# A two-layer diffusion trunk in one program: another instruction order, an output projection in eight blocks, another form for the weights' low parts

## The chip, the cores and the metric

The kernel runs on one core of a Trainium2 chip. The metric is the device time of one execution in microseconds (us); less is better. Times are medians of several executions; the profile is that of one execution, taken by the hardware profiler.

## The reference

One step through a trunk of two layers over 384 tokens (128 context, 256 latent), width 1024, everything in float32. A layer is a SwiGLU with half a residual, a token mixing of three head groups side by side, and a second SwiGLU; each is preceded by an RMS norm with a shift, a scale and a gate that come from a conditioning vector.

```python
def trunk_layer(x, mod, lp, lam_init, ctx=None, pos=None):
    sh1, sc1, g1, sh2, sc2, g2, sh3, sc3, g3 = (mod[:, i] for i in range(N_MOD))
    h = modulate(rms_norm(x, lp['g_norm'][0]), sh1, sc1)
    x = x + 0.5 * g1[:, None, :] * swiglu(h, lp['w_ffn_gate'][0], lp['w_ffn_up'][0], lp['w_ffn_down'][0])
    h = modulate(rms_norm(x, lp['g_norm'][1]), sh2, sc2)
    mix, new_ctx = token_mix(h, lp, lam_init, ctx, pos)
    x = x + g2[:, None, :] * mix
...
def token_mix(h, lp, lam_init, ctx, pos):
...
    out_c = diff_attention(c_q, keys_c, vals_c, lam)
    out_c = (rms_norm(out_c, lp['g_c_out']) * (1.0 - lam_init)).reshape(B, T, C_WIDTH)
    out = jnp.concatenate([out_a, out_b, out_c], axis=-1) @ lp['w_out']
```

Group a is grouped-query attention (384 columns of the concatenation), b a gated linear attention (256), c a differential attention of four heads of 96 columns (384): 1024 in all, eight times 128.

## The kernel before, in words

Six stages follow one another: FFN (0,0), mixing 0, FFN (0,1), FFN (1,0), mixing 1, FFN (1,1). Activations lie with features on the partitions and the 384 tokens along the free axis. Weights stream from memory in tiles of up to 128 x 1024. To keep float32 accuracy, every large product is three matmuls (`mm3`, L308 to L310): weight and activation are each split into a rounded high part and the rest. `load_split` does this for weights: a DMA on the SyncE queue (L299), the high part `whi` by ScalarE (L303), the low part `wlo = raw - whi` by VectorE (L304). Five raw buffers and three each of high and low parts stand in turn. While FFN stages run, VectorE also computes the conditioning vectors from `araw` tiles (L254).

At a stage's start TensorE begins with matmuls on `u`, the activation without its norm (`make_u`), since the norm's factor isn't known yet. `make_rstd` computes that factor: a matmul of ones on the summed squares `acc` (L377), a VectorE transpose (L379), three Newton steps on small tiles (`newton`, L315 to L327), a second transpose (L382). In mixing, `make_h` then makes the normed activation: GpSimd multiplies (L391), ScalarE writes the high part, VectorE shifts and scales (L397) and subtracts (L403). Projections onto 288, 384 and 512 columns (matmuls `<-whi,h`) need these; the four `t5` tiles (L604) are `u` products times the factor. In the FFN the first products are scaled by L464 and L469.

The mixing's second half is attention: queries times keys (L789 for group c), maximum (L694), exponential (L697), transposes (L721), values (L801, L803). `ORDER` gives the order in which the mixing's pieces are written for each layer. `c_first`, `c_next`, `c_norm` and `c_split` treat group c's output: two pairs of heads, each pair normed and split into four blocks of 96 rows in all.

The output projection multiplies nine blocks (three of a, two of b of 128 rows, four of c of 96 rows) for each of eight output tiles; `KORD` gives their order in the sum. Weights come in two loads a tile, of 640 and 512 columns. The order of instructions on an engine is what the tile framework's scheduler makes of the order in which they are written; each engine runs its queue in order.

Of the kernel before, what the change touches and what calls it, by code (L numbers as in the profile page):

```python
# [17 lines left out]
P = 128  # L18
D = 1024
KT = 8  # L20
SEQ = 128
LAT = 256
T = SEQ + LAT
# [23 lines left out]
TW = T + 2  # L47
# [7 lines left out]
NPT = 3  # L55
# [5 lines left out]
NRM = (0, 1)  # L61
HV = (1, 1, 1, 1, 1, 1, 1, 1)
ORDER = (
    ("ha br bq hb bk wq bv lg rq de wk st L0 rk L1 cx wa wv L2 c0 L3 c1 L4 c2 ra L5 L6 n0 s0 c3 n1 p0 ax "
     "s1 go o0 p1 p2 o1 o2").split(),
    ("br ha hb bq bk bv lg L0 wq rq wk de L1 st rk L2 wa cx wv L3 c0 ra L4 c1 c2 L5 c3 n0 L6 p0 ax "
     "go o0 p1 s0 p2 o1 n1 s1 o2").split(),
)
KORD = (
    ("c0 c1 c2 c3 b0 b1 a0 a1 a2").split(),  # L70
    ("a0 b0 b1 c0 c1 a1 c2 c3 a2").split(),
)


def build(tc, ins, outs):
    nc = tc.nc
    ctx = ExitStack()
    with ctx:
        _build(ctx, tc, nc, ins, outs)


def _build(ctx, tc, nc, I, O):
    V, S, G, PE = nc.vector, nc.scalar, nc.gpsimd, nc.tensor
# [3 lines left out]
    hp = ctx.enter_context(tc.tile_pool(name="hp", bufs=NHP))  # L87
# [208 lines left out]

    def load_split(src, cols=WCOL):
        raw = wp.tile([P, WCOL], F32, tag="wraw", bufs=NRAW, name="wraw")
        di = nc.sync.dma_start(out=raw[:, :cols] if len(src.shape) == 2 else  # L299
                               raw[:, :cols].rearrange("p (j c) -> p j c", j=src.shape[1]), in_=src)  # L300
# [260 lines left out]
    def mixing(l, us, acc, nxt):  # L561
        turn["own"] = {"mm": ("both",), "ax": ("ada",)}
        r_ = make_rstd(acc)
        with tc.tile_pool(name=f"mix{l}", bufs=1) as mp:
            def mt(shape, tag, bufs=1, dt=F32):
                return mp.tile(shape, dt, tag=tag, bufs=bufs, name=tag)
# [9 lines left out]
            s0 = mt([P, 2, 64], "s0")  # L576
# [6 lines left out]
            gco = sp[:, S_GCO + l:S_GCO + l + 1]  # L583
# [43 lines left out]
            c0, c1 = c01  # L627
# [107 lines left out]
            moa = []  # L735
# [14 lines left out]
            def a_out(i, pts):  # L750
                po = (mmps if PMM[6 + i] else axps)()[:, :T]
                for k in range(4):
                    for g in range(2):
                        r = slice(64 * g, 64 * g + 64)
                        if k == 0:
                            PE.matmul(po[r, 0:P], lhsT=av[:, 0, r], rhs=ptx[:, g, i, :], start=True, stop=True)
                        else:
                            PE.matmul(po[r, P:T], lhsT=av[:, k, r], rhs=pts[g][:, k - 1, :],  # L758
                                      start=(k == 1), stop=(k == 3))
                hi = hp.tile([P, TW], F32R, tag="h", name="ohi")[:, :T]  # L760
                S.activation(out=hi, in_=po, func=AF.Copy)
                lo = hp.tile([P, TW], F32R, tag="h", name="olo")[:, :T]
                V.tensor_tensor(out=lo, in0=po, in1=hi.bitcast(F32), op=ALU.subtract)
                moa.append((P, hi, lo))


            ptc_ = []
# [13 lines left out]
            moc = []  # L781
# [28 lines left out]
            cp = {}  # L810

            def c_first(j):
                cp[j] = mt([P, 2, T], "oc", 2)[:96], mt([P, 2, T], "pt", NPT)[:96], []
                c_next(j, 0)

            def c_next(j, i):
                oc, osq, pss = cp[j]
                c_head(2 * j + i, oc[:, i, :], osq[:, i, :], pss)

            def c_norm(j):  # L820
                oc, osq, pss = cp[j]
                r = rsq_bcast(mp, pss, T, 1.0 / 96, 96, "c", osq, osq)
                V.scalar_tensor_tensor(out=oc, in0=oc, scalar=gco[:96], in1=r, op0=ALU.mult, op1=ALU.mult)

            def c_split(j):
                oc = cp[j][0]
                for i in range(2):
                    hi = hp.tile([P, TW], F32R, tag="h", name="chi")[:96, :T]
                    S.activation(out=hi, in_=oc[:, i, :], func=AF.Copy)
                    lo = hp.tile([P, TW], F32R, tag="h", name="clo")[:96, :T]  # L830
                    V.tensor_tensor(out=lo, in0=oc[:, i, :], in1=hi.bitcast(F32), op=ALU.subtract)
                    moc.append((96, hi, lo))


            bv = mt([P, 3, 256], "bv")
            de = mt([P, 8, P], "de")
# [108 lines left out]
            def gla_out():  # L945
                ot = mt([P, 2, T], "e", 3)
                for i in range(2):
                    po = [(mmps if PMM[9] else axps)()[64 * j:64 * j + 64, :T] for j in range(2)]
                    for c in range(3):
                        for step in range(3 if c else 1):  # L950
                            for j in range(2):
                                h = 2 * i + j
                                r = slice(32 * h, 32 * h + 32)
                                pc = po[j][:, c * P:(c + 1) * P]
                                if step == 0:
                                    PE.matmul(pc, lhsT=bv[:, c, 64 * h:64 * h + 64], rhs=sc[i][:, j, c, :],
                                              start=True, stop=(c == 0))
                                elif step == 1:
                                    PE.matmul(pc, lhsT=s0[r, 0, :] if c == 1 else st[r, 0, :], rhs=de[r, c - 1, :],
                                              start=False, stop=False)  # L960
                                else:
                                    PE.matmul(pc, lhsT=st[r, 1, :] if c == 1 else s0[r, 1, :], rhs=de[r, c + 1, :],
                                              start=False, stop=True)
                    for j in range(2):
                        S.activation(out=ot[64 * j:64 * j + 64, i, :], in_=po[j], func=AF.Copy)
                oq = mt([P, 2, T], "e", 3)
                S.activation(out=oq, in_=ot, func=AF.Square)
                pss = []
                for i in range(2):
                    ps = (mmps if PMM[15] else axps)()[:, :T]  # L970
                    PE.matmul(ps, lhsT=bones, rhs=oq[:, i, :], start=True, stop=True)
                    pss.append(ps)
                r = rsq_bcast(mp, pss, T, 1.0 / 64, P, "b", oq, mt([P, 2, T], "e", 3))
                V.tensor_tensor(out=ot, in0=ot, in1=r, op=ALU.mult)
                V.scalar_tensor_tensor(out=ot, in0=ot, scalar=sp[:, S_GG + l:S_GG + l + 1], in1=sbr,
                                       op0=ALU.mult, op1=ALU.mult)
                for i in range(2):
                    hi = hp.tile([P, TW], F32R, tag="h", name="bhi")[:, :T]
                    lo = hp.tile([P, TW], F32R, tag="h", name="blo")[:, :T]
                    S.activation(out=hi, in_=ot[:, i, :], func=AF.Copy)  # L980
                    V.tensor_tensor(out=lo, in0=ot[:, i, :], in1=hi.bitcast(F32), op=ALU.subtract)
                    mob.append((P, hi, lo))

            sv = {}

# [81 lines left out]


            turn["own"] = {"mm": ("both",), "ax": ()}
            mo = [{"a": moa, "b": mob, "c": moc}[n[0]][int(n[1])] for n in KORD[l]]  # L1070
            acc = new_acc()
            us = []
            for m in range(KT):
                ps = mmps()[:, :T]
                for k0, k1 in ((0, 5), (5, 9)):
                    w = load_split(I["wo"][l, m][:, k0 * P:k1 * P], (k1 - k0) * P)
                    for k in range(k0, k1):
                        c = (k - k0) * P
                        n, hi, lo = mo[k]
# [139 lines left out]
```

## Time and profile before

| | us |
|---|---|
| median of 3 runs | 1598.27 (1590.26 to 1601.04) |
| profiled execution | 1599.75 |
| its span (first to last instruction) | 1597.9 |
| PE (TensorE) busy in it | 1563.3 |
| DVE (VectorE) busy | 1229.3 |
| ACT (ScalarE) busy | 738.8 |
| POOL (GpSimd) busy | 196.2 |

A busy share is an average over stages with different limits, so the stretches are to be looked at one by one. Matmuls overlap: one of 386 columns shows some 340 ns, while the next begins 175 ns after it. Where a stretch has fewer matmuls than its neighbours at the same busy time, the clock or the kind of matmul is another: PEclk is the TensorE clock that was granted, as a share of 2.4 GHz.

### The profile page before, as it was taken

The numbers are of one execution on the slowest core, as the hardware profiler recorded it, in microseconds if no ns is written. First come the engines' busy times: TensorE is split into PE (matmuls) and PEld (weight loads), VectorE is DVE, ScalarE is ACT, GpSimd is POOL, SyncE is SP. The second block draws the span as 40 slices with busy tenths as digits, with TensorE's granted clock in tenths as the row PEclk, the third lists the DMA queues.
The fourth block names the chain that finished last, engine by engine and source line by source line (L and its number), as shares of the span: only waits on it lengthen the run. The fifth ranks groups of instructions, "written<-read, shape, count | busy, mean of one in ns | idle before, by whom it ended". The sixth has DMA issues, their size and how long they took to land.

```text
span 1597.9 us, 25055 instructions
## 1 busy us (share of the span) xinstructions
PE 1563.3 (98%) x9370; PEld 1464.0 (92%) x9370; DVE 1229.3 (77%) x2294; ACT 738.8 (46%) x1444; POOL 196.2 (12%) x239
## 2 busy tenths in 40 slices
PE   7999999999999999999999999999999999999999
PEld 5999999997558999999999999999875699999999
DVE  4799999888766888898968889667787767666532
ACT  4544433365466544443344444335546754444321
POOL 1211130030000211111001111102000011111100
PEclk9999999999789999999999999999898999999999
DMA  9677778542104566666666666543321064443441
GB/s 330 231 229 229 226 225 261 165 122 83 45 1 140 168 197 202 201 192 207 204 213 197 210 197 195 174 144 96 113 77 39 1 230 144 143 137 130 120 143 57
DMA packets 83230, 256.38 MB, mean 160 GB/s; under 512 B 10978, under 2 KB 19746, under 8 KB 82722
## 3 DMA queue, kind: packets, MB, share of 16 engines
q1 hardware_dynamic: 83108, 254.78, 50.3%
q8 instruction: 74, 1.21, 0.3%
q14 instruction: 48, 0.39, 0.1%
HBM read 251.99 MB, written 2.75 MB: 159 GB/s over the span
## 4 chain that ended last, share of the span: by engine, by line
PE 90%; DVE 6%; ACT 2%; issue 1%; DMA 1%; POOL 1%; SPq 0%; DVEq 0%; ACTq 0%; POOLq 0%
PE mm L308 20%; PE mm L310 20%; PE mm L309 20%; PE both L308 7%; PE both L309 7%; PE both L310 7%; PE mm L789 1%; DVE wlo L304 1%; PE ax L803 1%; PE ax L901 1%; PE ax L721 1%; DVE junk L254 1%; PE ax L807 0%; DVE ht L397 0%; PE ax L758 0%
## 5 line engine op out<-in xcount | busy, mean ns | idle before, releaser
L303 ACT ACTIVATE whi<-wraw 128x1024 fp32r<-128x1024 f32 (+4 forms) x358 | 348.4, 975 | 461.2 <-PE mm L309 259.1
L304 DVE TENSOR_TENSOR wlo<-wraw,whi 128x1024 fp32r<-128x1024 f32 (+4 forms) x358 | 451.8, 1264 | 131.0 <-ACT whi L303 129.0
L310 PE MATMUL mm<-h,wlo 128*128 128x386 f32 x1096 | 373.3, 341 | 2.5 <-DVE wlo L304 2.5
L308 PE MATMUL mm<-h,whi 128*128 128x386 f32 x1096 | 372.8, 341 | 2.6 <-POOL h L367 1.4
L309 PE MATMUL mm<-h,whi 128*128 128x386 f32 x1096 | 372.5, 340 | 0.0
L254 DVE SCALAR_TENSOR_TENSOR junk<-araw,cb 128x1024 f32<-128x1024 f32 x256 | 312.3, 1220 | 0.8
L310 PEld LDWEIGHTS mm<-h,wlo 128*128 128x128 f32 x1096 | 208.0, 190 | 4.2 <-DVE wlo L304 3.5
L308 PEld LDWEIGHTS mm<-h,whi 128*128 128x128 f32 x1096 | 207.6, 190 | 4.6 <-ACT whi L303 1.7
L309 PEld LDWEIGHTS mm<-h,whi 128*128 128x128 f32 x1096 | 207.6, 189 | 1.6 <-issue 0.7
L477 POOL TENSOR_TENSOR alo<-s,ahi 128x384 fp32r<-128x384 f32 x88 | 115.5, 1314 | 641.5 <-ACT ahi L475 614.9
L309 PE MATMUL mm<-alo,whi 128*128 128x384 f32 x528 | 177.9, 337 | 0.0
L310 PE MATMUL mm<-ahi,wlo 128*128 128x384 f32 x528 | 177.9, 337 | 0.0
L308 PE MATMUL mm<-ahi,whi 128*128 128x384 f32 x528 | 177.9, 337 | 0.0
L308 PE MATMUL both<-h,whi 128*128 128x386 f32 x360 | 122.5, 340 | 0.0
L309 PE MATMUL both<-h,whi 128*128 128x386 f32 x360 | 122.1, 339 | 0.0
L310 PE MATMUL both<-h,wlo 128*128 128x386 f32 x360 | 122.0, 339 | 0.0
L475 ACT ACTIVATE ahi<-s 128x384 fp32r<-128x384 f32 x88 | 46.3, 526 | 129.4 <-DVE s L472 129.3
L309 PEld LDWEIGHTS mm<-alo,whi 128*128 128x128 f32 x528 | 99.2, 188 | 0.0
L310 PEld LDWEIGHTS mm<-ahi,wlo 128*128 128x128 f32 x528 | 99.2, 188 | 0.0
L308 PEld LDWEIGHTS mm<-ahi,whi 128*128 128x128 f32 x528 | 99.2, 188 | 0.0
L469 DVE TENSOR_TENSOR u<-mm,rstd 128x384 f32<-128x384 f32 x66 | 36.6, 554 | 60.8 <-PE mm L310 60.8
L467 ACT ACTIVATE s<-s,bc 128x128 f32<-128x128 f32 (+1 forms) x176 | 70.7, 449 | 8.0 <-ACT bc L418 0.7
(365 smaller groups left out, 2446.7 us busy)
## 6 DMA issues: line engine op xcount, KB each, us to landing
wraw<-in_wgu SPq DMA_DIRECT2D x170, 512.0 KB, 4.2
araw<-in_w_adat SPq DMA_DIRECT2D x128, 512.0 KB, 4.0
wraw<-in_wd SPq DMA_DIRECT2D x64, 512.0 KB, 4.2
wraw<-in_wd SPq DMA_DIRECT2D x32, 384.0 KB, 3.5
araw<-in_w SPq DMA_DIRECT2D x16, 512.0 KB, 5.6
wraw<-in_wo SPq DMA_DIRECT2D x16, 320.0 KB, 3.0
wraw<-in_wit SPq DMA_DIRECT2D x8, 512.0 KB, 3.4
wraw<-in_wa SPq DMA_DIRECT2D x8, 512.0 KB, 3.6
```

The lines of the kernel that those rows point to most:

```text
L254: V.scalar_tensor_tensor(out=junk, in0=w, scalar=1.0, in1=self.cb[:, c, :], op0=ALU.mult, op1=ALU.mult, accum_out=self.acc[:, f, c:c + 1])
L303: S.activation(out=hi[:, :cols], in_=raw[:, :cols], func=AF.Copy)
L304: vi = V.tensor_tensor(out=lo[:, :cols], in0=raw[:, :cols], in1=hi[:, :cols].bitcast(F32), op=ALU.subtract)
L308: PE.matmul(ps, lhsT=lh, rhs=rh, start=start, stop=False)
L309: PE.matmul(ps, lhsT=lh, rhs=rl, start=False, stop=False)
L310: return PE.matmul(ps, lhsT=ll, rhs=rh, start=False, stop=stop)
L467: S.activation(out=s[:, a:b], in_=s[:, a:b], func=AF.Silu, bias=bg[:, c:c + 1])
L469: vi = V.tensor_tensor(out=u, in0=pu[:, :T], in1=r, op=ALU.mult)
L475: S.activation(out=hi, in_=s, func=AF.Copy)
L477: G.tensor_tensor(out=lo, in0=s, in1=hi.bitcast(F32), op=ALU.subtract)
L721: pi = PE.transpose(ps[:, i * P:(i + 1) * P], p[:, i, :], ident)
L789: PE.matmul(pp[m], lhsT=qtc[r, h, (t + 1) * P:(t + 2) * P], rhs=ktc[r, h, 0:T], start=True, stop=True)
```

## The change

Five edits. The whole kernel is built in an inner tile context whose scheduler picks each next instruction along a simulated timeline. `ORDER` and `KORD` are other lists. The output projection has eight blocks of 128 rows: the fourth c head's 96 rows are laid as three times 32 rows under the other three heads' 96. Its weights come by loads of 512 columns, and the load whose blocks hold c's is three DMAs. `wlo` is made by SCALAR_TENSOR_TENSOR (times 1.0, minus) instead of TENSOR_TENSOR.

```diff
...
-     "go o0 p1 s0 p2 o1 n1 s1 o2").split(),
+     "go n1 o0 p1 s0 p2 s1 o1 o2").split(),
...
 KORD = (
-    ("c0 c1 c2 c3 b0 b1 a0 a1 a2").split(),
-    ("a0 b0 b1 c0 c1 a1 c2 c3 a2").split(),
+    ("c0 c1 c2 b0 b1 a0 a1 a2 c3").split(),
+    ("a0 b0 b1 a1 c0 c1 c2 a2 c3").split(),
 )
 def build(tc, ins, outs):
     nc = tc.nc
-    ctx = ExitStack()
-    with ctx:
-        _build(ctx, tc, nc, ins, outs)
+    with tc.tile_critical(), tile.TileContext(nc, schedule_with_timeline_sim=True) as inner, ExitStack() as ctx:
+        _build(ctx, inner, nc, ins, outs)
...
-        vi = V.tensor_tensor(out=lo[:, :cols], in0=raw[:, :cols], in1=hi[:, :cols].bitcast(F32), op=ALU.subtract)
+        vi = V.scalar_tensor_tensor(out=lo[:, :cols], in0=raw[:, :cols], scalar=1.0, in1=hi[:, :cols].bitcast(F32),
+                                    op0=ALU.mult, op1=ALU.subtract)
...
             def c_norm(j):
                 oc, osq, pss = cp[j]
                 r = rsq_bcast(mp, pss, T, 1.0 / 96, 96, "c", osq, osq)
-                V.scalar_tensor_tensor(out=oc, in0=oc, scalar=gco[:96], in1=r, op0=ALU.mult, op1=ALU.mult)
+                n = 2 - j
+                V.scalar_tensor_tensor(out=oc[:96, :n], in0=oc[:96, :n], scalar=gco[:96], in1=r[:, :n],
+                                       op0=ALU.mult, op1=ALU.mult)
+                if j:
+                    for i in range(3):
+                        q = slice(32 * i, 32 * i + 32)
+                        V.scalar_tensor_tensor(out=cp[i // 2][0][96:P, i % 2, :], in0=oc[q, 1, :], scalar=gco[q],
+                                               in1=r[q, 1, :], op0=ALU.mult, op1=ALU.mult)
...
             for m in range(KT):
                 ps = mmps()[:, :T]
-                for k0, k1 in ((0, 5), (5, 9)):
-                    w = load_split(I["wo"][l, m][:, k0 * P:k1 * P], (k1 - k0) * P)
+                for k0, k1 in ((0, 4), (4, 8)):
+                    w = load_split(wo_parts(I["wo"][l, m], k0, k1), (k1 - k0) * P)
...
-                        mm3(ps, w[0][:n, c:c + P], w[1][:n, c:c + P], hi, lo, k == 0, k == 8)
+                        hi, lo = mo[k]
+                        mm3(ps, w[0][:, c:c + P], w[1][:, c:c + P], hi, lo, k == 0, k == KT - 1)
```

`wo_parts` names the three pieces: 96 rows of all columns, 32 rows of the three c blocks' columns (from the fourth head's rows), 32 rows of the one other block. In the changed file `load_split` and everything behind it stands a few lines lower: L306 is the old L304, L311 to L313 the old L308 to L310, L380 the old L377, L385 the old L382, L400 the old L397, L406 the old L403, L607 the old L604.

TensorE's queue at the start of mixing 0 (`mm` and `both` are the first two of the four `u` products, their eighths in the order of `h`; `acc` is the sum of squares), before:

```order
L308 MATMUL mm_3374<-h_3150,whi_3370 128x386
L309 MATMUL mm_3374<-h_3151,whi_3370 128x386
L377 MATMUL ada_3267<-acc_2362,cst_85 128x384
L310 MATMUL mm_3374<-h_3150,wlo_3371 128x386
L308 MATMUL mm_3374<-h_3255,whi_3370 128x386
L309 MATMUL mm_3374<-h_3256,whi_3370 128x386
L310 MATMUL mm_3374<-h_3255,wlo_3371 128x386
L308 MATMUL both_3411<-h_2464,whi_3407 128x386
```

and after:

```order
L311 MATMUL both_3419<-h_2930,whi_3415 128x386
L312 MATMUL both_3419<-h_2931,whi_3415 128x386
L313 MATMUL both_3419<-h_2930,wlo_3416 128x386
L312 MATMUL mm_3382<-h_3264,whi_3378 128x386
L313 MATMUL mm_3382<-h_3263,wlo_3379 128x386
L311 MATMUL both_3419<-h_3042,whi_3415 128x386
L380 MATMUL ada_3275<-acc_2370,cst_93 128x384
L312 MATMUL both_3419<-h_3043,whi_3415 128x386
```

The ones matmul stood in the seventh eighth of the first product, behind 20 matmuls of the stage; it stands in the sixth eighth of the second, behind 40.

VectorE's queue at the same place, from inside the Newton steps to the first normed block, before:

```order
L327 SCALAR_TENSOR_TENSOR ny_3282<-na_3279,ny_3275 128x12
L304 TENSOR_TENSOR wlo_3522<-wraw_3519,whi_3521 128x1024
L324 TENSOR_TENSOR na_3284<-ny_3282 128x12
L325 TENSOR_TENSOR na_3284<-na_3284,nh_3277 128x12
L327 SCALAR_TENSOR_TENSOR ny_3287<-na_3284,ny_3282 128x12
L324 TENSOR_TENSOR na_3289<-ny_3287 128x12
L325 TENSOR_TENSOR na_3289<-na_3289,nh_3277 128x12
L327 SCALAR_TENSOR_TENSOR ny_3292<-na_3289,ny_3287 128x12
L382 STREAM_TRANSPOSE rstd_3294<-ny_3292 128x384
L604 TENSOR_TENSOR t5_3399<-mm_3374,rstd_3294 128x384
L397 TENSOR_SCALAR ht_3328<-ht_3331,ae01_2017,mod3_99 128x128
```

and after, first right behind the first transpose:

```order
L306 SCALAR_TENSOR_TENSOR wlo_3530<-wraw_3527,whi_3529 128x1024
L318 TENSOR_SCALAR nm_3279<-ht_3277 128x12
L320 TENSOR_SCALAR ns_3281<-nm_3279 128x12
L324 TENSOR_SCALAR nh_3285<-nm_3279 128x12
L306 SCALAR_TENSOR_TENSOR wlo_3570<-wraw_3567,whi_3569 128x768
L322 TENSOR_SCALAR ny_3283<-ns_3281 128x12
```

then behind the Newton steps:

```order
L385 STREAM_TRANSPOSE rstd_3302<-ny_3300 128x384
L306 SCALAR_TENSOR_TENSOR wlo_3594<-wraw_3591,whi_3593 128x768
L607 TENSOR_TENSOR t5_3407<-mm_3382,rstd_3302 128x384
L607 TENSOR_TENSOR t5_3444<-both_3419,rstd_3302 128x384
L607 TENSOR_TENSOR t5_3481<-mm_3456,rstd_3302 128x384
L400 TENSOR_SCALAR ht_3336<-ht_3339,ae01_2025,mod3_107 128x128
```

One weight part stood among the Newton steps, now two do; one `t5` product stood between the factor and the first L397, now a third weight part and three `t5` products do.

SyncE's queue at the first loads of the output projection of mixing 0, before:

```order
L299 DMA wraw_5398<-in_wo 128x640
L299 DMA wraw_5419<-in_wo 128x512
L299 DMA wraw_5441<-in_wo 128x640
L299 DMA wraw_5462<-in_wo 128x512
L299 DMA wraw_5486<-in_wo 128x640
```

and after:

```order
L302 DMA wraw_5405<-in_wo 96x512
L302 DMA wraw_5405<-in_wo 32x3x128
L302 DMA wraw_5405<-in_wo 32x128
L302 DMA wraw_5425<-in_wo 128x512
L302 DMA wraw_5447<-in_wo 96x512
```

An output tile's weights were two DMAs and are four.

## Rows read from the trace of the kernel before

**Rows 1.** The page: span and instructions; busy us and share of each engine.
```profile
span 1597.9 us, 25055 instructions
PE 1563.3 (98%) x9370; PEld 1464.0 (92%) x9370; DVE 1229.3 (77%) x2294; ACT 738.8 (46%) x1444; POOL 196.2 (12%) x239
```
**Rows 2.** The page: shares of the span in the chain that ended last.
```profile
PE 90%; DVE 6%; ACT 2%; issue 1%; DMA 1%; POOL 1%; SPq 0%; DVEq 0%; ACTq 0%; POOLq 0%
```
**Rows 3.** Stretches of 50 us: length, busy us (x instructions) per engine, PEclk, DMA share, GB/s.
```profile
0.00:50.00 50.00, 39.89 (x266) 28.42 (x267) 24.20 (x58) 24.07 (x46) 8.37 (x23) 1.00 0.88 315
...
100.00:150.00 50.00, 50.00 (x285) 50.00 (x284) 49.12 (x75) 21.08 (x39) 8.27 (x6) 1.00 0.72 227
...
350.00:400.00 50.00, 48.15 (x397) 40.00 (x397) 44.07 (x105) 32.21 (x72) 6.44 (x8) 0.97 0.33 98
400.00:450.00 50.00, 47.07 (x258) 28.79 (x258) 36.24 (x95) 23.22 (x57) 3.05 (x2) 0.73 0.13 36
...
1100.00:1150.00 50.00, 46.88 (x329) 43.78 (x328) 38.22 (x85) 33.44 (x75) 10.07 (x10) 0.90 0.33 97
...
1200.00:1250.00 50.00, 48.21 (x352) 29.03 (x351) 38.46 (x114) 31.90 (x86) 4.21 (x5) 0.86 0.09 26
```
**Rows 4.** Instructions of single lines by form: count, duration ns min/median/max.
```profile
L308 PE MATMUL mm<-chi,whi x48: 331/338/442, 487.9 to 1309.2; 96*128 96x384 f32 x48
L308 PE MATMUL mm<-ohi,whi x36: 333/338/445, 495.1 to 1309.7; 128*128 128x384 f32 x36
...
L304 DVE TENSOR_TENSOR wlo<-wraw,whi x358: 678/1216/2040, 12.3 to 1583.7; 128x1024 fp32r<-128x1024 f32 x129, 128x768 fp32r<-128x768 f32 x24, 128x640 fp32r<-128x640 f32 x16, 128x512 fp32r<-128x512 f32 x6
...
L254 DVE SCALAR_TENSOR_TENSOR junk<-araw,cb x256: 1206/1215/1915, 73.5 to 1479.7; 128x1024 f32<-128x1024 f32 x128
```
**Rows 5.** DMA issues: KB each, median us from issue to landing.
```profile
wraw<-in_wo SPq DMA_DIRECT2D x16, 320.0 KB, 3.0
...
wraw<-in_wo SPq DMA_DIRECT2D x16, 256.0 KB, 3.0
```
**Rows 6.** PE's timeline at the start of mixing 0: start us, duration us.
```profile
311.10 0.34 PE L308 MATMUL mm<-h,whi 128*128 128x386 f32 x1
...
314.65 0.89 PE L377 MATMUL ada<-acc,cst 128*128 128x384 f32 x2
```
**Rows 7.** DVE's timeline at the start of mixing 0; in brackets idle before.
```profile
315.57 0.58 DVE L379 STREAM_TRANSPOSE ht<-ada 128x384 f32<-128x384 f32 x1 [1.00 <-PE ada L377]
...
319.70 0.58 DVE L382 STREAM_TRANSPOSE rstd<-ny 128x384 f32<-128x384 f32 x1
320.31 0.56 DVE L604 TENSOR_TENSOR t<-mm,rstd 128x384 f32<-128x384 f32 x1
321.47 1.93 DVE L397 TENSOR_SCALAR ht<-ht,ae,mod 128x128 f32<-128x128 f32 x4 [0.60 <-POOL ht L391]
...
323.79 0.90 DVE L403 TENSOR_TENSOR h<-ht,h 128x384 fp32r<-128x384 f32 x1
324.61 0.94 DVE L304 TENSOR_TENSOR wlo<-wraw,whi 128x768 fp32r<-128x768 f32 x1
```
**Rows 8.** PE's timeline, the two longest waits of the mixings' first halves and heads of c.
```profile
420.65 1.96 PE L789 MATMUL mm<-ktc,qtc 64*128 64x384 f32 x4 [2.46 <-ACT p L697]
...
1117.05 0.40 PE L309 MATMUL mm<-wlo,h 128*128 128x288 f32 x1 [1.88 <-DVE wlo L304]
```
**Rows 9.** Stretches of 10 us behind the wait that ends at 420.65 us; columns as in rows 3.
```profile
420.00:430.00 10.00, 8.88 (x21) 4.45 (x22) 7.87 (x26) 6.81 (x19) 0.00 (x0) 0.58 0.10 28
430.00:440.00 10.00, 10.00 (x53) 4.87 (x54) 4.57 (x13) 4.01 (x12) 0.00 (x0) 0.50 0.00 0
440.00:450.00 10.00, 10.00 (x63) 5.48 (x65) 5.24 (x16) 5.38 (x14) 0.00 (x0) 0.56 0.00 0
```
**Rows 10.** DVE's timeline at the start of FFN (0,1), behind the output projection.
```profile
536.88 2.42 DVE L369 SCALAR_TENSOR_TENSOR h<-x,ae,h 128x256 fp32r<-128x256 f32 x7
...
544.28 0.55 DVE L464 TENSOR_TENSOR s<-mm,rstd 128x384 f32<-128x384 f32 x1
```

More of the change, by code (lines that the diff above doesn't have):

```diff
@@ L63 @@
 ORDER = (
-    ("ha br bq hb bk wq bv lg rq de wk st L0 rk L1 cx wa wv L2 c0 L3 c1 L4 c2 ra L5 L6 n0 s0 c3 n1 p0 ax "
-     "s1 go o0 p1 p2 o1 o2").split(),
+    ("ha br bq hb bk wq bv lg rq de wk st L0 rk L1 cx wa wv L2 c0 L3 c1 L4 c2 ra L5 L6 n0 c3 n1 p0 ax "
+     "s0 s1 go o0 p1 p2 o1 o2").split(),
     ("br ha hb bq bk bv lg L0 wq rq wk de L1 st rk L2 wa cx wv L3 c0 ra L4 c1 c2 L5 c3 n0 L6 p0 ax "
-     "go o0 p1 s0 p2 o1 n1 s1 o2").split(),
+     "go n1 o0 p1 s0 p2 s1 o1 o2").split(),
 )
 KORD = (
-    ("c0 c1 c2 c3 b0 b1 a0 a1 a2").split(),
-    ("a0 b0 b1 c0 c1 a1 c2 c3 a2").split(),
+    ("c0 c1 c2 b0 b1 a0 a1 a2 c3").split(),
+    ("a0 b0 b1 a1 c0 c1 c2 a2 c3").split(),
 )
@@ L298, in load_split @@
         raw = wp.tile([P, WCOL], F32, tag="wraw", bufs=NRAW, name="wraw")
-        di = nc.sync.dma_start(out=raw[:, :cols] if len(src.shape) == 2 else
-                               raw[:, :cols].rearrange("p (j c) -> p j c", j=src.shape[1]), in_=src)
+        for rows, cs, part in (src if isinstance(src, list) else [(slice(0, P), slice(0, cols), src)]):
+            dst = raw[rows, cs]
+            if len(part.shape) == 3:
+                dst = dst.rearrange("p (j c) -> p j c", j=part.shape[1])
+            di = nc.sync.dma_start(out=dst, in_=part)
         hi = wp.tile([P, WCOL], F32R, tag="whi", bufs=3, name="whi")
@@ L763, in a_out @@
                 V.tensor_tensor(out=lo, in0=po, in1=hi.bitcast(F32), op=ALU.subtract)
-                moa.append((P, hi, lo))
+                moa.append((hi, lo))
             ptc_ = []
@@ L812, in c_first @@
             def c_first(j):
-                cp[j] = mt([P, 2, T], "oc", 2)[:96], mt([P, 2, T], "pt", NPT)[:96], []
+                cp[j] = mt([P, 2, T], "oc", 2), mt([P, 2, T], "pt", NPT)[:96], []
                 c_next(j, 0)
@@ L817, in c_next @@
                 oc, osq, pss = cp[j]
-                c_head(2 * j + i, oc[:, i, :], osq[:, i, :], pss)
+                c_head(2 * j + i, oc[:96, i, :], osq[:, i, :], pss)
             def c_norm(j):
@@ L822, in c_norm @@
                 r = rsq_bcast(mp, pss, T, 1.0 / 96, 96, "c", osq, osq)
-                V.scalar_tensor_tensor(out=oc, in0=oc, scalar=gco[:96], in1=r, op0=ALU.mult, op1=ALU.mult)
-            def c_split(j):
[L826 to L832, printed above, removed]
+                n = 2 - j
[6 more added lines that the diff above has]
+                                               in1=r[q, 1, :], op0=ALU.mult, op1=ALU.mult)
+            def c_split(j):
+                for i in range(2 - j):
+                    oc = cp[j][0][:, i, :]
+                    hi = hp.tile([P, TW], F32R, tag="h", name="chi")[:, :T]
+                    S.activation(out=hi, in_=oc, func=AF.Copy)
+                    lo = hp.tile([P, TW], F32R, tag="h", name="clo")[:, :T]
+                    V.tensor_tensor(out=lo, in0=oc, in1=hi.bitcast(F32), op=ALU.subtract)
+                    moc.append((hi, lo))
             bv = mt([P, 3, 256], "bv")
@@ L981, in gla_out @@
                     V.tensor_tensor(out=lo, in0=ot[:, i, :], in1=hi.bitcast(F32), op=ALU.subtract)
-                    mob.append((P, hi, lo))
+                    mob.append((hi, lo))
             sv = {}
@@ L1069, in mixing, with wo_parts @@
             turn["own"] = {"mm": ("both",), "ax": ()}
-            mo = [{"a": moa, "b": mob, "c": moc}[n[0]][int(n[1])] for n in KORD[l]]
+            mo = [{"a": moa, "b": mob, "c": moc}[n[0]][int(n[1])] for n in KORD[l][:KT]]
+            kc = KORD[l].index("c0")
+            def wo_parts(w, k0, k1):
+                if not k0 <= kc < k1:
+                    return w[:, k0 * P:k1 * P]
+                b = (kc - k0) * P
+                parts = [(slice(0, 96), slice(0, (k1 - k0) * P), w[0:96, k0 * P:k1 * P]),
+                         (slice(96, P), slice(b, b + 3 * P),
+                          w[0:96, KT * P:(KT + 1) * P].rearrange("(j p) c -> p j c", j=3))]
+                for k in range(k0, k1):
+                    if not kc <= k < kc + 3:
+                        parts.append((slice(96, P), slice((k - k0) * P, (k - k0 + 1) * P), w[96:P, k * P:(k + 1) * P]))
+                return parts
             acc = new_acc()
@@ L1074, in mixing @@
                 ps = mmps()[:, :T]
-                for k0, k1 in ((0, 5), (5, 9)):
-                    w = load_split(I["wo"][l, m][:, k0 * P:k1 * P], (k1 - k0) * P)
+                for k0, k1 in ((0, 4), (4, 8)):
+                    w = load_split(wo_parts(I["wo"][l, m], k0, k1), (k1 - k0) * P)
                     for k in range(k0, k1):
                         c = (k - k0) * P
-                        n, hi, lo = mo[k]
-                        mm3(ps, w[0][:n, c:c + P], w[1][:n, c:c + P], hi, lo, k == 0, k == 8)
+                        hi, lo = mo[k]
+                        mm3(ps, w[0][:, c:c + P], w[1][:, c:c + P], hi, lo, k == 0, k == KT - 1)
                 end_tile(l, 1, m, ps, acc, nxt, None)
```

## The prediction

> **What bounds the kernel now.** I read the page's busy shares first, then the shares of the chain that ended last, then stretches of 50 us. TensorE is busy for 1563.3 of 1597.9 us [rows 1], and the chain runs over it for 90% [rows 2]. In an FFN stage the limit is plain: 50.00 of 50 us busy at full clock, 285 matmuls [rows 3], so one matmul of 384 or 386 columns costs 50/285 = 0.175 us. VectorE is nearly full there as well (49.12 of 50 us in that stretch), which the page's mean of 77% hides.
>
> Where time can be won is seen in the other stretches of the same table [rows 3]. The start has 10 us in which TensorE isn't busy. The mixings have 2 to 3 us of idle per 50 us, and they lose more by the clock: with a granted share of 0.73 the stretch from 400 to 450 us loses 0.27 x 50 = 13.5 us, with 0.90 and 0.86 two stretches of mixing 1 lose 5 and 7 us. The timeline shows what came before the longest of these: TensorE waited 2.46 us for the first exponentials of group c's heads [rows 8], and then worked for 30 us at 0.50 to 0.58 of the clock, which is the lower level of 1.2 GHz, while busy nearly all the time [rows 9]. So in the FFN stages only fewer matmuls count; in the mixings the order counts, by idle time and by the clock.
>
> **The output projection.** Per layer 9 x 3 x 8 = 216 matmuls become 192. A block of 96 rows costs what one of 128 costs (medians of 338 ns each) [rows 4], so a block less is a gain of its whole price: 48 x 0.175 = 8.4 us over two layers where TensorE is the limit. Some of the projection is written as filler among the attention's last pieces: counted in the two queues, 56 of the 216 matmuls stand ahead of the last attention matmul before, 45 of 192 after. If fillers stand in time that would be idle anyway, only those behind count: 160 - 147 = 13 per layer, 4.6 us in all. I take 8.4 and keep 4.6 as the other end. Group c's norm becomes four VectorE instructions in place of one; a 384-column VectorE operation shows some 0.55 us [rows 7], so this adds up to 1.5 us per layer. It lies in the attention, where TensorE has other heads' work; at nothing, or 3 us if that cover is gone.
>
> The loads: 64 DMAs instead of 32, at some 3.0 us to landing [rows 5]. One load now feeds 12 matmuls, 2.1 us; five raw buffers hold 10 us of work, more than three landings. So nothing, and if the pieces landed as late as the slowest weight loads of the profile the first tile would wait about 2 us per layer. The Trainium skill speaks against this edit: "SBUF — State Buffer", section "The DMA setup-cost knee", asks for 128 partitions and one transfer as large as can be where transfers bind. Here they don't bind in the trace (the share of DMA engines in the stretches before is 0.13 and less) [rows 3], and the sum is the same by either.
>
> **The weights' low parts.** 358 instructions change form. VectorE's nearest rows: TENSOR_TENSOR of 1024 columns 1216 ns median, SCALAR_TENSOR_TENSOR of 1024 columns from two buffers 1215 ns [rows 4]. At nothing; the forms' extremes (1206 and 2040) come from waiting beside GpSimd's work and bound neither. Were it 5% slower, 20 us of VectorE would be added, and the stretch with 49.12 of 50 us busy would pay some 10 of them; were it 5% faster nothing much would follow, since TensorE is full there.
>
> **The order at a mixing's start.** Here the change moves work on the path. Before, with the first `u` matmul at 311.10 as zero [rows 6], the ones matmul came at 3.55 us, behind 20 matmuls. Its transpose started at 4.47, the second transpose ended at 9.2 (4.71 us for the chain with one weight part in it), the first L397 ran at 10.4, and the first normed block was there at 13.6 [rows 7]. TensorE had some 100 matmuls of `u` work till about 17.5 us, so it never waited. After, the ones matmul stands behind 40: 7.0 us. Transpose 7.9; chain 4.71 plus a second weight part of 768 columns, 0.9 net: 13.5. Then another part (0.9) and three `t5` products in place of one (3 x 0.47 = 1.4): 15.8; four L397 (1.9) and L403 (0.9): 18.6. TensorE's queue reaches the first matmul that needs it at 96 x 0.175 + 0.9 = 17.7, so it waits about 1.1 us. The second block stands behind a `t5` product of the last `u` tile and comes at about 22.6: 2.1 us more. The third and fourth cost some 0.8 each. Sum 4.8 us, against 0.2 to 0.3 before in mixing 0: +4.5. In mixing 1 the queues have the same form, and TensorE already waited 1.88 us for a weight part [rows 8]; if the new stall replaces that, +3. Bounds: nothing (if the stall is taken out of waits that come later, as that at 418 us) and 6 us each.
>
> **The order at FFN starts behind the projection.** The ones matmul moves from 14 to 53 matmuls in: 9.3 us. From it to L464 it took 8.8 us with seven L369 (2.42) between [rows 10]; these now stand ahead of it, and one weight part more (1.2) stands in the chain: 9.3 + 8.8 - 2.4 + 1.2 = 16.9, with the product and the bias columns 18.3. TensorE wants the first bank again 100 matmuls in, at 17.5. So +0.8 for each of two stages; bounds 0 and 3.
>
> **The rest of the order.** In the FFNs' steady stretches TensorE's queue is the same, so nothing. In the attention group c's first exponential still stands behind two weight parts and other elementwise work on VectorE, at the same depth of both queues; I take the wait of 2.46 us and the slow clock behind it as staying, with -20 (both slow stretches gone: 13.5 + 7) as the far end. At the start two groups of loads change places while the DMA engines' share is 0.88 [rows 3]: the same bytes, 0 with 3 us either way.
>
> **The inner context.** It adds a semaphore round at the start and a second set of drains and barriers at the end. The profile doesn't show these. What lies around the span now, with one such ending in it, is 1599.75 - 1597.9 = 1.85 us; I take 2, bounds 0 and 6 (three times that).
>
> **Sum.** -8.4 + 4.5 + 3 + 1.6 + 2 = +2.7. On the profiled execution's own 1599.75 that gives 1602.4; it lies 1.5 us over the median of the runs, so a median of 1601.
>
> **Rivals.** *The order mends the slow clock.* The matmuls of 512 columns that stood in one run of 78 are now mixed with small ones, and more of the queries' products stand ahead, so the wait before 420.65 could go; against it speaks that VectorE, nearly full up to that place, has no less to do. Price: 13.5 + 7 us back, and the starts' 9.1 us not paid if VectorE keeps up: 1601 - 20.5 = 1580.5, down to 1571. It decides if the granted clock of 420 to 450 us is 1.0.
>
> *The late factor drops the clock at the mixings' starts* (the slower side). In the trace a wait of 1.88 us at 1115 us was followed by a clock of 0.90 over its 50 us, and one of 2.46 us by the 30 us at half [rows 3, 8, 9]. The new stall of 1.1 and 2.1 us close together is of that size. A fall as long as the one at 420 costs 13.5 us in mixing 0; in mixing 1, which has 5 us of it now, 8.5 more: 1615 for one, 1623 for both. It decides if TensorE waits more than about 2 us in one piece at the first normed blocks. The Trainium skill, in "TensorE: Matmul & The Clock Gate", section "HAM oscillation", describes this: a wait between two bursts of matmuls throttles the engine, and the next burst starts cold. The trace agrees at 420 us, where the clock fell after the wait; behind the shorter wait of mixing 1 it fell for less of the time.
>
> *The order moves nothing that counts.* The stalls come out of later waits: -8.4 + 2, 1592. *The projection's gain is hidden*: 4.6 for 8.4, 1605.
>
> **Chances.** A change of less than 1% (16 us) is about what a measurement of this kernel can tell from none. The forecast with its near neighbours, from 1587 to 1612: 0.53. The mended clock: 0.30, nearly all of it below 1582, since one slow stretch alone with no stall gives 1601 - 13.5 - 9.1 = 1578. The fallen clock: 0.17, most of it above 1614. So faster 0.29, same 0.53, slower 0.18. The range leaves out about one in ten at either end: 1575 to 1617; the likeliest case's own is 1587 to 1612.
>
> **What would show it.** Right: the ones matmul of mixing 0 about 7 us after the first `u` matmul, TensorE waiting 3 to 6 us in the first 20 us of each mixing, 192 projection matmuls at 0.175 us, low parts of 1024 columns at 1.21 us, the slow stretch behind the first exponentials still there. Wrong: no wait at the normed blocks, a granted clock of 1.0 through the attention, a low part that isn't at 1.2 us, or a gap of more than 5 us between span and execution time.

## The result, and the profile after

The changed kernel takes 1619.51 us (median of 4 runs, 1611.19 to 1626.45) against 1594.26 us for the kernel before on the same chip: a ratio of 1.015, 95% interval 1.0108 to 1.0192. It is slower by some 25 us. The prediction was 1601 us with a range from 1575 to 1617; faster, same and slower had chances of 0.29, 0.53 and 0.18.

The profiled execution is the longest of the four, 1626.45 us. Its page answers to [rows 1] and [rows 2]:

```profile
span 1624.6 us, 25158 instructions
PE 1571.9 (97%) x9322; PEld 1466.6 (90%) x9322; DVE 1205.5 (74%) x2298; ACT 731.1 (45%) x1442; POOL 204.1 (13%) x239
...
PE 88%; DVE 6%; ACT 2%; issue 2%; DMA 1%; POOL 0%; SPq 0%; DVEq 0%; POOLq 0%; ACTq 0%
```

There are 48 matmuls fewer (9370 to 9322) and yet 8.6 us more of busy TensorE. Busy time grows while work shrinks, and the mean granted clock of this execution is 0.966, against 0.980 in the profile of the kernel before. Stretches of 50 us, with the columns of [rows 3], show where:

```profile
0.00:50.00 50.00, 36.01 (x226) 25.21 (x230) 20.36 (x46) 21.38 (x40) 5.43 (x18) 0.97 0.81 293
...
100.00:150.00 50.00, 50.00 (x284) 50.00 (x284) 49.97 (x79) 21.76 (x42) 8.56 (x6) 1.00 0.69 227
...
400.00:450.00 50.00, 42.14 (x297) 28.26 (x292) 41.22 (x111) 26.39 (x72) 6.35 (x3) 0.80 0.11 34
450.00:500.00 50.00, 46.21 (x333) 28.89 (x331) 28.98 (x95) 28.10 (x79) 2.40 (x6) 0.66 0.01 1
500.00:550.00 50.00, 48.69 (x253) 38.58 (x253) 26.76 (x64) 25.94 (x53) 0.00 (x0) 0.90 0.41 140
...
1200.00:1250.00 50.00, 46.77 (x283) 33.94 (x281) 42.68 (x104) 27.25 (x68) 6.21 (x4) 0.90 0.20 55
```

The FFN's steady state is what it was (100 to 150 us). The first 50 us hold 40 matmuls fewer. The attention of mixing 0 (400 to 550 us) is the place: TensorE is idle for longer in it (busy for 42.14 us from 400 to 450 us, against 47.07 before [rows 3]), and the clock is low for longer.

Taking both traces stage by stage, from the start of one stage's matmuls to the next, the 26.7 us between the two spans lie like this: start and FFN (0,0) +5.1; mixing 0 +16.2, of which +8.8 in the projections, +14.9 from there to the last attention matmul, and -7.5 in what is left of the output projection (138 matmuls behind the last attention matmul instead of 187); the two FFNs between +1.7; mixing 1 +0.9; FFN (1,1) and the end +2.8. In mixing 1 what the shorter projection gives is lost again.

### The profile page after: what moved, and what is told of

Read it like the earlier page. It is cut to its first block, busy times and chain, and to the rows that moved or that the text cites. A ratio compares the mean times of both kernels' runs of the same rounds, so it can differ in the third digit from the quotient of the medians.

```text
span 1624.6 us, 25158 instructions
## 1 busy us (share of the span) xinstructions
PE 1571.9 (97%) x9322; PEld 1466.6 (90%) x9322; DVE 1205.5 (74%) x2298; ACT 731.1 (45%) x1442; POOL 204.1 (13%) x239
## 4 chain that ended last, share of the span: by engine, by line
PE 88%; DVE 6%; ACT 2%; issue 2%; DMA 1%; POOL 0%; SPq 0%; DVEq 0%; POOLq 0%; ACTq 0%
PE mm L311 20%; PE mm L313 20%; PE mm L312 19%; PE both L311 7%; PE both L313 7%; PE both L312 7%; DVE wlo L306 1%; PE mm L792 1%; PE ax L724 1%; PE ax L806 1%; PE ax L912 1%; ACT p L700 1%; PE ada L166 0%; DMA araw<-in_w 0%; ACT whi L305 0%
## 5 line engine op out<-in xcount | busy, mean ns | idle before, releaser
L305 ACT ACTIVATE whi<-wraw 128x1024 fp32r<-128x1024 f32 (+3 forms) x358 | 346.6, 971 | 585.3 <-PE mm L312 342.7
L306 DVE SCALAR_TENSOR_TENSOR wlo<-wraw,whi 128x1024 fp32r<-128x1024 f32 (+3 forms) x358 | 413.6, 1156 | 140.4 <-ACT whi L305 137.6
L311 PE MATMUL mm<-h,whi 128*128 128x386 f32 x1096 | 370.6, 341 | 6.6 <-ACT h L369 3.6
L313 PE MATMUL mm<-h,wlo 128*128 128x386 f32 x1096 | 372.4, 340 | 0.3 <-DVE wlo L306 0.3
L253 DVE SCALAR_TENSOR_TENSOR junk<-araw,cb 128x1024 f32<-128x1024 f32 x256 | 317.6, 1240 | 0.6
L311 PEld LDWEIGHTS mm<-h,whi 128*128 128x128 f32 x1096 | 207.3, 190 | 9.8 <-POOL h L374 4.5
L313 PEld LDWEIGHTS mm<-h,wlo 128*128 128x128 f32 x1096 | 207.2, 189 | 1.6 <-DVE wlo L306 1.0
L480 POOL TENSOR_TENSOR alo<-s,ahi 128x384 fp32r<-128x384 f32 x88 | 119.4, 1356 | 634.8 <-ACT ahi L478 543.1
L311 PE MATMUL mm<-ahi,whi 128*128 128x384 f32 x528 | 177.9, 337 | 0.0
L313 PE MATMUL mm<-ahi,wlo 128*128 128x384 f32 x528 | 177.9, 337 | 0.0
L313 PE MATMUL both<-h,wlo 128*128 128x386 f32 x360 | 122.2, 339 | 0.2 <-DVE wlo L306 0.2
L311 PE MATMUL both<-h,whi 128*128 128x386 f32 x360 | 122.3, 340 | 0.0
L311 PEld LDWEIGHTS mm<-ahi,whi 128*128 128x128 f32 x528 | 99.2, 188 | 0.0
L313 PEld LDWEIGHTS mm<-ahi,wlo 128*128 128x128 f32 x528 | 99.2, 188 | 0.0
```

Of the source, the lines that this page charges most:

```text
L253: V.scalar_tensor_tensor(out=junk, in0=w, scalar=1.0, in1=self.cb[:, c, :], op0=ALU.mult, op1=ALU.mult, accum_out=self.acc[:, f, c:c + 1])
L306: vi = V.scalar_tensor_tensor(out=lo[:, :cols], in0=raw[:, :cols], scalar=1.0, in1=hi[:, :cols].bitcast(F32), op0=ALU.mult, op1=ALU.subtract)
L480: G.tensor_tensor(out=lo, in0=s, in1=hi.bitcast(F32), op=ALU.subtract)
```

## The experiments

Each was timed beside the kernel before on the same chip. First, each edit alone.

**Eight blocks alone (e1_wo8).** The kernel before with the new projection; the two lists go with it, since the fourth head's rows are written by the second norm into the tiles that the first split reads.

```diff
+            def wo_parts(w, k0, k1):
...
-                for k0, k1 in ((0, 5), (5, 9)):
-                    w = load_split(I["wo"][l, m][:, k0 * P:k1 * P], (k1 - k0) * P)
+                for k0, k1 in ((0, 4), (4, 8)):
+                    w = load_split(wo_parts(I["wo"][l, m], k0, k1), (k1 - k0) * P)
```

> The kernel before with the output projection over 8 blocks and the two lists that go with it, ordinary scheduling, low parts as before. Theory A (the simulated order costs the time): 4 to 8 us below before, 1586 to 1590, since 48 matmuls of 0.175 us go. Theory B (the 8 blocks cost: every block of c now waits for all four heads, and the lists move the attention's pieces): 10 to 25 us above before, and half-clock time in mixing 0 near the 68 us of the changed kernel instead of 34.

Measured: 1586.3 us against 1594.52, ratio 0.9938 (0.9915 to 0.9961). Theory A's number, and theory B falls. Both mixings are shorter in the profiled executions (213.6 and 216.6 us from the first `u` matmul to the last of the projection; 222.1 and 223.2 before), but these ran at mean granted clocks of 0.985 and 0.980, so a part of that difference is the clock's. At one clock, 0.985, the kernel before took 1593.1 to 1594.5 us in this set of runs and this kernel 1585.5 to 1586.7: some 8 us less.

**The fused form alone (e2_fused).**

```diff
-        vi = V.tensor_tensor(out=lo[:, :cols], in0=raw[:, :cols], in1=hi[:, :cols].bitcast(F32), op=ALU.subtract)
+        vi = V.scalar_tensor_tensor(out=lo[:, :cols], in0=raw[:, :cols], scalar=1.0, in1=hi[:, :cols].bitcast(F32),
+                                    op0=ALU.mult, op1=ALU.subtract)
```

> The kernel before with the low parts by SCALAR_TENSOR_TENSOR alone; the same order on every engine. Both theories: within 3 us of before, 1594 to 1600; low parts of 1024 columns at 1.21 us as before. Theory C (the fused form itself is dearer where VectorE is full): 5 us or more above, and FFN (0,0) longer by that.

Measured: 1589.47 us, ratio 0.9973 (0.9949 to 0.9997). The line's row, to set beside that of the old form in [rows 4] (count, ns min/median/max):

```profile
L304 DVE SCALAR_TENSOR_TENSOR wlo<-wraw,whi x358: 679/1218/2040, 13.3 to 1577.9; 128x1024 fp32r<-128x1024 f32 x129, 128x768 fp32r<-128x768 f32 x24, 128x640 fp32r<-128x640 f32 x16, 128x512 fp32r<-128x512 f32 x6
```

1218 against 1216 ns: the two forms cost the same. The median's few us are then not the form's; the runs of this kernel granted TensorE 0.988 of its clock in eight of ten, and the kernel before, with the same order, takes 1589 us too where it gets 0.988, and 1600 us at 0.980.

**The inner context with ordinary scheduling (e4_ctx), and with the simulated order (e3_sim).** The kernel before, built as in the change, once without and once with the option.

```diff
-    ctx = ExitStack()
-    with ctx:
-        _build(ctx, tc, nc, ins, outs)
+    with tc.tile_critical(), tile.TileContext(nc) as inner, ExitStack() as ctx:
+        _build(ctx, inner, nc, ins, outs)
```

> The kernel before in the inner context with the ordinary scheduler: order as before on every engine. All theories: 1 to 3 us above before, of which 1.3 at the end behind the last output DMA and 0.3 at the first instructions; stages between as long as before.

Measured: 1598.11 us, ratio 1.0026 (1.0002 to 1.0051). By the medians that is 3.6 us, a little more than expected, though the interval (0.3 to 8 us) holds the expectation too; and it lies at another place. The first FFN matmul comes 2.7 us later, the last of FFN (0,0) 4.4 us later; the 1.7 us between are the clock's (granted 0.96 and 0.87 in the two stretches from 30 to 50 us, 1.00 before). SyncE's timeline shows where the 2.7 us come from, before:

```profile
1.82 1.77 SPq L165 DMA_DIRECT2D araw<-in_w  x4
...
601.51 0.33 SPq L246 DMA_DIRECT2D araw<-in_w_adat  x1
```

and in the inner context:

```profile
2.86 2.54 SPq L164 DMA_DIRECT2D araw<-in_w  x4
...
599.81 0.47 SPq L245 DMA_DIRECT2D araw<-in_w_adat  x1
```

Issuing a DMA takes longer there from the start (2.54 us for four instead of 1.77) through the middle (0.47 us instead of 0.33) to the last output (again 0.47 and 0.33). Only at the start does TensorE wait for loads: 8.7 us in all, against 5.9 before.

> The kernel before in the inner context whose scheduler follows the simulated timeline; projection, lists and low parts as before. Theory A: 25 to 35 us above before (the changed kernel's 25 plus the 8 us that 8 blocks would give), with about 5 us lost by the end of FFN (0,0) and half-clock time over 60 us in mixing 0. Theory B: within 8 us of before.

Measured: 1636.97 us, ratio 1.0252 (1.0203 to 1.0302). So the simulated order costs 39 us over the context alone in the kernel before. The changed kernel, which has the 8 blocks, their lists and the fused form besides, is 17 us faster than that.

**The changed kernel without inner context and order (e5_after_plain).**

```diff
-    with tc.tile_critical(), tile.TileContext(nc, schedule_with_timeline_sim=True) as inner, ExitStack() as ctx:
-        _build(ctx, inner, nc, ins, outs)
+    ctx = ExitStack()
+    with ctx:
+        _build(ctx, tc, nc, ins, outs)
```

> The changed kernel without the inner context and its simulated order: 8 blocks, their lists and the fused low parts stay, ordinary scheduling. If the order and its context hold the whole loss: 1582 to 1589, as the run with 8 blocks alone. If 8 blocks and fused form together cost something that neither does alone: above 1592.

Measured: 1586.93 us, the kernel before beside it 1589.6, ratio 0.9976 (0.9952 to 0.9999). The same time as 8 blocks alone, though the kernel before is only 2.7 us slower here: ten of its nineteen executions got a clock of 0.988 or more. At 0.985 it took 1593.4 and 1594.0 us, this kernel 1585.9 to 1586.8, so at one clock the 8 blocks gain some 7.5 us here too. The whole loss is the order's and its context's: 1619.5 against 1587, 32 us by the medians, 28 by the two ratios. The changed kernel wasn't timed again beside this run and those that follow, and its own four executions spread over 15 us; differences from its 1619.5 are to be read with that in mind.

Then, which part of the order. Each of the next six keeps the changed kernel and its scheduler, but ties a chosen set of instructions on each engine to the order in which the ordinary scheduler has them; everything else stays free. The ties order the issue and wait for nothing.

```diff
+PIN = (
+    ("PE", "..."),
...
+def pin(tc, nc):
+    at = {i.name: i for i in nc.cur_bb.bb.instructions}
+    for _, d in PIN:
...
+                tc.add_manual_dep(i, prev.name, mybir.DependencyInfo(mybir.DependencyClass.NoSync,
+                                  mybir.DependencyReason.DATA), reason="pin")
...
         _build(ctx, inner, nc, ins, outs)
+        pin(inner, nc)
```

**Both mixings (h1_pin_mix), and mixing 0 alone (h6_pin_mix0).** `PIN` holds all instructions that the mixings write, on all five engines.

> The changed kernel with the simulated order, but all instructions traced in the two mixings keep, among themselves and on each engine, the ordinary scheduler's order. If the loss lies in the mixings' order: 1588 to 1595 (the 8-block kernel and the 4 us of the context). If it lies in the FFN stages, in the start or in how the stages overlap: above 1605.

Measured: 1588.23 us, ratio 0.996 (0.9929 to 0.999).

> The changed kernel with all engines held to the ordinary order in mixing 0 alone. The traces put 25 us of the loss against the 8-block kernel into mixing 0 and 8 into mixing 1: 1592 to 1600. If the two mixings share the loss evenly: 1603 to 1608.

Measured: 1593.85 us, ratio 0.9995 (0.9968 to 1.0023). The loss is in the mixings, 26 of 31 us in mixing 0. What is left of the simulated order, in FFNs and start, costs nothing that can be told from the context's cost.

**The first part, the second part (h2_pin_proj, h3_pin_att).** `PIN` holds the norm's factor, normed blocks and projections, or linear attention, softmaxes, values and norms.

> The changed kernel with the ordinary order only for the mixings' first part: the norm's factor, the normed blocks, the projections. The late ones matmul (theory: first cause, the attention's slow clock follows from it): 1590 to 1600. If the first part costs only its own stalls, some 8 and 5 us: 1603 to 1610. If it doesn't matter: 1615 to 1622.

> The changed kernel with the ordinary order only for the mixings' second part: linear attention, softmaxes, values, c's norm and split. If the attention's own order costs its 15 us in mixing 0 and 12 in mixing 1: 1592 to 1602. If the attention is late and slow because of the late first part: 1610 to 1622.

Measured: 1612.31 us (1.0121, 1.0085 to 1.0157) and 1625.07 us (1.0216, 1.0167 to 1.0266). Neither part alone brings the time back. The intervals of both overlap that of the changed kernel (1.0108 to 1.0192), so 7 us and nothing are what the medians say, and no more; they don't add up to the 31 us of both together. How the two parts are laid between each other stays free in both runs, so it may be there that the rest lies; no run held that alone. With the second part held, it runs faster (73.9 us from the last projection matmul of mixing 0 to the last attention matmul, at a granted clock of 0.98; 98.8 us at 0.72 in the changed kernel), but the first part grows by 13 us.

**TensorE alone, the others alone (h4_pin_pe, h5_pin_others).**

> The changed kernel with TensorE alone held to the ordinary order inside both mixings; VectorE, ScalarE, GpSimd and SyncE keep what the simulated order makes beside it. If TensorE's own order makes the waits and the slow clock: 1585 to 1597, near the kernel with all engines held (1588). If the other engines' order makes them: above 1610.

> The changed kernel with the four other engines held to the ordinary order inside both mixings, TensorE free. If TensorE's own order makes the waits: above 1610. If the other engines' order makes them: 1585 to 1597.

Measured: 1623.91 us (1.0186, 1.0141 to 1.023) and 1651.47 us (1.0373, 1.0323 to 1.0423). By its own conditions each of the two runs blames the engines that it leaves free, and the two contradict each other, so neither theory holds: neither TensorE's own order nor that of the others makes the loss by itself. The first mixture of the two schedules is as slow as the changed kernel, within the intervals, and the second is clearly slower than both.

**The starts alone (h7_pin_start).** `PIN` holds the ones matmul with its Newton steps, the normed blocks and the `u` products.

> The changed kernel with only the mixings' starts held to the ordinary order: the ones matmul, the Newton steps, the normed blocks and the u products. The prediction's term for this was 7.5 us over both mixings. If it is paid as a stall: 1610 to 1616. If the late factor is what drops the clock later: below 1605. If the stall comes out of later waits: 1617 to 1622.

Measured: 1603.6 us, ratio 1.0049 (1.0021 to 1.0077): 16 us below the changed kernel. The start's small set is worth half of the loss, far more than its stalls. Whole mixing 0 of five kernels, from the first `u` matmul to the last of the projection, columns as in [rows 3]; the kernel before (24 matmuls more):

```profile
311.10:533.22 222.12, 215.16 (x1443) 171.34 (x1443) 168.10 (x428) 133.09 (x299) 27.06 (x35) 0.92 0.29 91
```

the changed kernel:

```profile
316.17:554.50 238.33, 222.98 (x1419) 173.86 (x1419) 169.77 (x433) 132.05 (x302) 28.36 (x36) 0.86 0.26 81
```

with only the starts held:

```profile
316.40:538.10 221.70, 206.36 (x1419) 166.05 (x1419) 170.40 (x433) 131.94 (x302) 27.70 (x36) 0.91 0.28 87
```

with both mixings held:

```profile
313.70:523.60 209.90, 203.72 (x1419) 162.63 (x1418) 167.94 (x431) 131.96 (x300) 26.91 (x36) 0.96 0.30 93
```

and 8 blocks, ordinary scheduling, fused form (e5_after_plain):

```profile
312.80:526.50 213.70, 207.58 (x1420) 164.26 (x1419) 168.51 (x432) 132.34 (x300) 27.00 (x35) 0.94 0.30 92
```

In the last four the same 1419 matmuls take 209.9 to 238.3 us. Idle TensorE is length less busy: 15.4, 15.3, 6.2 and 6.1 us. What the clock takes can be estimated as (1 - granted) x length: 33, 20, 8 and 13 us. The starts' order took 13 us off the clock's share and nothing off the idle time.

## Why the prediction was wrong

**Right as worked out.** *The 48 matmuls*: 8.4 us; the run with 8 blocks alone is 8.2 us lower by its medians, and at one granted clock 7.5 to 8 us are gained in both runs that have the 8 blocks and ordinary scheduling. A block of 96 rows had indeed cost what one of 128 does. The other end, 4.6, came from a wrong count: in mixing 0 the traces have 29 of 216 projection matmuls ahead of the last attention matmul before and 54 of 192 after, in mixing 1 21 and none, not 56 and 45 in each. *The four DMAs* for a tile cost nothing: in the run with 8 blocks alone TensorE waits in the projections for 0.42 us and 1.19 us, both times for a block of activations (the second wait was there before), and never for a load. *The fused form*: nothing, as the nearest rows said. *The times of a mixing's start* came as walked through; VectorE's timeline of the changed kernel, beside [rows 7]:

```profile
324.11 0.58 DVE L382 STREAM_TRANSPOSE ht<-ada 128x384 f32<-128x384 f32 x1 [4.46 <-PE ada L380]
...
329.21 0.58 DVE L385 STREAM_TRANSPOSE rstd<-ny 128x384 f32<-128x384 f32 x1
...
333.08 1.23 DVE L400 TENSOR_SCALAR ht<-ht,ae,mod 128x128 f32<-128x128 f32 x4
334.24 0.55 DVE L406 TENSOR_TENSOR h<-ht,h 128x384 fp32r<-128x384 f32 x1
```

With the first `u` matmul at 316.18 us the transpose starts at 7.9 (forecast 7.9), the factor is there at 13.6 (13.5), the first normed block at 18.6 (18.6). VectorE's wait for the ones matmul grew from 1.00 to 4.46 us, which is 20 matmuls of 0.175 us. The last of these agreements is in part luck: the first L400 starts at 16.9, not 15.8, and from there the four L400 and the L406 take 1.7 us together, not 2.8.

**Mis-sized.** *The stall* that follows was put at 4.8 us for a mixing. It is one wait of 2.39 us in mixing 0, for the second block (the first, third and fourth came in time), and 2.4 us in three pieces in mixing 1. TensorE reached the first normed block at 17.7 us as forecast, but six matmuls there need only the block's high part:

```profile
333.84 0.34 PE L311 MATMUL mm<-whi,h 128*128 128x384 f32 x1
...
334.89 0.38 PE L313 MATMUL mm<-whi,h 128*128 128x384 f32 x1
```

The first of the low part starts at 334.89, 18.7 us in, and by then the block is there. *The context* was put at 2 us, at both ends; it is 3.6 by the medians, with 2.7 us at the start, where issuing DMAs takes longer. *FFN starts*: 0.8 us each; TensorE waits 1.2 us in each of the two (1.03 and 0.16). Added to what they replace, these terms were 11.1 us in the sum, and measured they come to some 9: with them the sum would have been about zero.

**The step that failed** is "The rest of the order": that the attention would stay as it was, with the wait of 2.46 us and the slow clock behind it, and could only gain. It was put at nothing; the other terms as measured leave nearly the whole 25 us to it, and with both mixings held to the ordinary order 31 us were gone. It was read from the depth of the two queues at the first exponentials alone. In mixing 0 of the kernel before TensorE waited for 1 us and more twice, for 2.46 us [rows 8] and here:

```profile
477.46 0.91 PE L744 MATMUL both<-kta,qta 64*128 64x384 f32 x2 [1.62 <-ACT e L965]
```

Its waits of 1 us and more in mixing 0 of the changed kernel:

```profile
339.37 0.47 PE L313 MATMUL mm<-whi,h 128*128 128x384 f32 x1 [2.39 <-DVE h L406]
...
410.37 0.90 PE L912 MATMUL ada<-e 32*64 32x64 f32 x12 [3.19 <-ACT t L712]
...
433.37 1.47 PE L792 MATMUL mm<-ktc,qtc 64*128 64x384 f32 x4 [1.84 <-ACT p L700]
...
438.53 0.90 PE L724 MATMUL ax<-cst,p 128*128 128x128 f32 x3 [1.25 <-DVE p L800]
471.84 0.87 PE L724 MATMUL ax<-cst,p 128*128 128x128 f32 x6 [1.35 <-DVE sd L948]
473.91 2.87 PE L806 MATMUL ada<-pt,cv 128*96 128x256 f32 x6 [1.20 <-ACT pt L725]
496.53 2.62 PE L747 MATMUL mm<-kta,qta 64*128 64x384 f32 x4 [1.10 <-ACT p L700]
```

Seven such waits instead of two, and 15.4 us of idle TensorE in all instead of 7.0. And the clock, in stretches of 10 us as in [rows 9]:

```profile
340.00:350.00 10.00, 10.00 (x51) 9.72 (x50) 9.10 (x18) 5.84 (x11) 3.82 (x3) 0.85 0.35 104
...
410.00:420.00 10.00, 8.65 (x34) 6.91 (x35) 9.62 (x33) 3.29 (x13) 0.00 (x0) 0.59 0.01 2
...
430.00:440.00 10.00, 6.73 (x24) 3.24 (x23) 8.47 (x25) 6.39 (x17) 0.00 (x0) 0.76 0.18 56
440.00:450.00 10.00, 10.00 (x56) 4.96 (x58) 6.96 (x21) 6.49 (x19) 0.00 (x0) 0.73 0.01 2
450.00:460.00 10.00, 10.00 (x66) 5.72 (x68) 5.41 (x18) 5.63 (x16) 0.00 (x0) 0.66 0.00 1
...
470.00:480.00 10.00, 7.46 (x68) 4.80 (x59) 2.37 (x10) 5.73 (x16) 2.40 (x6) 0.64 0.01 2
480.00:490.00 10.00, 10.00 (x50) 6.66 (x46) 2.96 (x15) 2.94 (x6) 0.00 (x0) 0.50 0.00 0
490.00:500.00 10.00, 8.90 (x28) 4.69 (x26) 9.14 (x23) 8.52 (x29) 0.00 (x0) 0.50 0.01 2
500.00:510.00 10.00, 10.00 (x28) 4.18 (x29) 4.72 (x18) 1.86 (x4) 0.00 (x0) 0.50 0.00 0
```

The slow stretch behind the first exponentials is still there, in two pieces (436 to 446 and 453 to 459 us, 17 us against 27 before); the one from 473 to 510 us, 37 us at 0.50, is new.

Against the same kernel under ordinary scheduling, mixing 0 has 9.2 us more idle and 20 us more lost to the clock, for 24.6 us more length (some of the waiting would pass at either clock, so the two don't simply add). Mixing 1 is 7.7 us longer than there.

**The rivals.** "The mended clock" held nothing. "The late factor drops the clock" had the sign, and a falling clock is most of the loss. Its place was wrong, and that its 1615 lies near the median of 1619.5 is luck. At 340 us, right behind the 2.39 us wait, the clock was at 0.50 for only some 3 us. The long fall begins at 473 us, as TensorE comes from a wait of 1.35 us and goes into one of 1.20 us; the wait at 496 us lies inside it. That the order of the starts has a part in the loss is shown: only the starts put back gave 16 of the 32 us, by the clock's share. How a delay travels from the start to 410 and 473 us was not followed: the starts' pins hold more than the ones matmul and also move what is free beside them, so the part of the late factor alone stays open.

Nor is every fall shown to come from a wait. In stretches of 1 us the clock falls at 408 us inside the wait of 3.19 us, at 436 us some 2 us behind that of 1.84 us, and at 473 us between two waits. But at 453 us it falls with no wait behind it: from 440 to 460 us TensorE is busy throughout, in the rows above. What made it fall there stays open. The Trainium skill's description in "TensorE: Matmul & The Clock Gate", section "HAM oscillation", that waits between bursts throttle the engine, agrees with the first three of these falls and not with the fourth; it speaks of waits for data from memory, and here they are for ScalarE and VectorE.

**The chances.** The 0.18 for slower rested on one long wait at the start as the only trigger. The price of such a wait was known from the trace of before: 27 us of half clock in mixing 0 behind the single wait of 2.46 us, the 13.5 us of the rival. With an order that was rewritten through the whole attention, more such waits were as likely as fewer.

## What to carry to other kernels

Where TensorE is busy nearly all the time, a wait's price is not its length: look at the granted clock of the stretch behind it. Here 2.39 us at a start cost some 1.5 us of clock, and two waits of 1.35 and 1.20 us in the attention stood at the head of 37 us at half clock. A reordering is to be judged by the waits it leaves in the stages where engines take turns, as in attention, and there one part of a schedule couldn't be valued without the rest: holding TensorE's order alone, or that of the others alone, was as slow as the changed kernel or slower, and all engines together gave back 31 us. An edit that removes instructions from the full engine (8 blocks: 0.9938 alone, 0.9976 with the fused form) can be had without the scheduler that came with it.

## What the runs showed that was not expected

The same program's time follows the clock it happens to get: the changed kernel's four executions took 1611.19, 1618.59, 1620.42 and 1626.45 us at mean granted clocks of 0.978, 0.973, 0.970 and 0.966, with the same instructions in the same order. A step of 0.012 in the mean is 15 us; 0.012 of 1620 us would be 19. So a single profile of such a kernel says less about its time than several runs' clocks do, and two kernels are best compared at one clock too: beside the 8 blocks the kernel before was 8.2 us slower by the medians in one set of runs and 2.7 in another, and 7.5 to 8 in both at 0.985.

Issuing the same DMA took 0.47 us of SyncE's time in the inner context and 0.33 outside, with no other edit. It mattered only where TensorE waited for loads, here in the first 15 us.
